# Gate and branch projections of a gated mixer, turned: tokens on the output partitions, 512 weight columns streaming, and the mixture transposed for the output projection

## The chip, the cores and the metric

The kernel runs on one core of one Trainium2 chip. The metric is the device time of one execution in microseconds (us), the median of three runs. Of the core's engines, TensorE (PE) multiplies and transposes, VectorE (DVE) and ScalarE (ACT) do the elementwise work, and SyncE (SP) issues the transfers of the weights. PSUM, into which TensorE writes, has eight banks of 128 partitions x 512 four-byte numbers.

## The reference

A trunk of two layers on 256 tokens of width 1024. Each layer has four residual steps, each behind a layer norm: a feed-forward half step, three gated mixers side by side, a cross attention to a memory, and a second feed-forward half step. The change is in the mixers:

```python
y_a = nsa_mixer(...)      # native sparse attention, 8 heads, width 512
y_b = hgrn2_mixer(...)    # gated linear recurrence, 4 heads, width 512
y_c = mla_mixer(...)      # latent attention, 8 heads, width 512
gates = sigmoid(merge.reshape(B, S, 3, D_MODEL))      # merge = x @ w_in's last 3072 columns
mixed = (gates[:, :, 0] * (y_a @ w_branch[l, 0]) + gates[:, :, 1] * (y_b @ w_branch[l, 1])
         + gates[:, :, 2] * (y_c @ w_branch[l, 2]))   # 256 x 1024
x = layer_norm(alpha * x + mixed @ w_out[l], ln_g[l, 1], ln_b[l, 1])
```

So each layer has three gate projections (256 x 1024 by 1024 x 1024), three branch projections (256 x 512 by 512 x 1024) and one output projection (256 x 1024 by 1024 x 1024) of the mixture.

## The kernel before

**Products.** Every factor is held as two fp32r tiles, a high part and the rest (names ending in h and l), and each product is three matmuls into the same PSUM region: high by high, high by low, low by high. They are issued by `mm3`, lines 127, 128 and 129, so each of these lines does a third of almost every product. Weights come in blocks of 128 x 1024 (512 KB): SP loads `raw` (5 buffers), ScalarE rounds it to `wh` (line 77) and VectorE makes the rest, `wl` (line 78), with 4 buffers each. VectorE so has one 128x1024 instruction for every block that TensorE works through.

**Gates and branches.** `merge(i, fc)` computes 128 of the 1024 gate columns of mixer i (0 is a, 1 is b, 2 is c): eight steps over k, the weight tile of 128 x 128 stationary and the 256 tokens of `xT` moving, so that the result `mg` has gate columns on the partitions and tokens along the row. ScalarE turns it to tanh in `th` (line 508). `branch(i, fp)` does the same for 256 of the 1024 columns of a branch projection (`br`, four steps over k), and VectorE forms (th + 1) * br; mixer b, the first, writes `mixed` (line 520), a and c go through `th` and are added (lines 523 and 524). With the last one, c, each 128 columns of `mixed` are at once halved and split into `mh` and `ml` (lines 528 and 529). In this layout `mixed` is already what the output projection needs as its stationary side. PSUM comes from two pools of four banks, `pacc` (mg, br of a and b, the output `y`) and `ppw` (scores, transposes, br of c).

**What stands around them.** Gates and branches are also the work that fills TensorE while the attention units wait for their softmax. They stand in the list `fillers`, and `fill(n)` takes the next n. Attention runs in 12 units (0 to 7 are heads of mixer a, 8 to 11 pairs of heads of c). The scores of a unit (`s`, lines 827 and 829) are issued two units ahead by `soft`, which also issues its softmax: VectorE masks and takes the maximum (line 427), ScalarE exponentiates (line 431), VectorE takes the reciprocal, applies the gate and scales `p` (lines 433, 435, 438). `unit(u, n)` then is:

```python
fill(n)                        # n = FILLS[u]
pT = flip(ahead.pop(0))        # six transposes of p (line 446), copies of them
if u == 0: ...                 # two transposes of scm (line 950), copied to pc
ahead.append(soften_a(u + 2))  # the scores of the unit after next
values_a(u, pT)                # oa <- pc, vc (line 841) and pT, vs (line 456)
```

`scm` is the softmax over compressed keys, for all heads at once, from `psc` (line 927), through VectorE's lines 929 to 940. The order of the text isn't the order on the engines: a scheduler lays each engine's instructions out ahead of the run, by times that it estimates.

**The tail of the mixers.** After unit 11 and the remaining fillers come `branch(2, fp)` for fp 0 to 3, two gates of c between them, and `nat_out`, the output projection: `y` in four banks, `mh` stationary and 512 columns of `w_out` moving, eight steps over k. `load_mem` loads the next step's memory beside it, with VectorE's `memT` (line 78, 128x512).

Of the kernel before, what the change touches and what calls it, by code (L numbers as in the profile page):

```python
# [30 lines left out]
ROPE_THETA = 500000.0  # L31
NEG = -1e30
TRAIL = 3
FILLS = (7, 0, 0, 0, 1, 2, 2, 2, 4, 4, 4, 0)
LEVELS = (4, 8, 16, 32, 64)
C_ID, C_CAUS, C_BASE, C_HM, C_CM, C_CM1, C_INV, C_END = 0, 128, 384, 448, 456, 488, 520, 536

# [2 lines left out]
def trunk(ctx, tc, a, out):  # L40
# [90 lines left out]
    def cut(hl, *idx):  # L131
        return tuple(t[idx] for t in hl)
# [331 lines left out]
    def mixer(l, xT, first, pre):  # L464
# [27 lines left out]
            return yh[name]  # L492


        order = "bac"
        mixed = []
        th = {}

        def merge(i, fc):
            ps = pacc([P, S], "mg")  # L500
            mode_b(ps, wblock(a["winb"][l, 8 + i * 8 + fc]), xT)
            if order[-1] == "abc"[i]:
                if fc % 4 == 0:
                    th[i] = big([P, 4, S], name="th")
                th[i, fc] = th[i][:, fc % 4, :]
            else:
                th[i, fc] = wk.tile([P, S], F32, tag="s", name="th", bufs=3)
            A.activation(th[i, fc], ps, AF.Tanh, scale=0.5)

        def branch(i, fp):  # L510
            w = wblock(a["wbr"][l, i, fp])
            res = []
            for u in range(2):
                fc = fp * 2 + u
                ps = (ppw if order[-1] == "abc"[i] else pacc)([P, S], "br")
                mode_b(ps, cut(w, slice(None), slice(u * 512, (u + 1) * 512)), yh["abc"[i]], 4)
                if order[0] == "abc"[i]:
                    if fc % 4 == 0:
                        mixed.append(big([P, 4, S], name="mixed"))
                    V.scalar_tensor_tensor(mixed[fc // 4][:, fc % 4, :], th[i, fc], 1.0, ps, op0=ALU.add, op1=ALU.mult)  # L520
                    continue
                m = mixed[fc // 4][:, fc % 4, :]
                V.scalar_tensor_tensor(th[i, fc], th[i, fc], 1.0, ps, op0=ALU.add, op1=ALU.mult)
                V.tensor_tensor(m, m, th[i, fc], op=ALU.add)
                if order[-1] == "abc"[i]:
                    mh = wk.tile([P, S], F32R, tag="gh", name="mh", bufs=4)
                    ml = wk.tile([P, S], F32R, tag="gl", name="ml", bufs=4)
                    A.activation(mh, m, AF.Copy, scale=0.5)
                    V.scalar_tensor_tensor(ml, m, 0.5, f(mh), op0=ALU.mult, op1=ALU.subtract)
                    res.append((mh, ml))  # L530
            return res

        def gated(i):
            u = []
            for fp in range(4):
                u += [lambda fp=fp: merge(i, fp * 2), lambda fp=fp: merge(i, fp * 2 + 1), lambda fp=fp: branch(i, fp)]
            return u

        fillers = []
# [222 lines left out]
            V.scalar_tensor_tensor(hx, u, 1.0, hx, op0=ALU.add, op1=ALU.mult)  # L762
            gel.append(hx)

        fillers += [lambda fc=fc: merge(2, fc) for fc in range(6)]
        compress(0)
        hgrn_out(0)
        blocks(1)
# [204 lines left out]
        memT = [load_mem(0)]  # L973

        ys = [[pacc([P, 512], "y") for _ in range(2)] for _ in range(NT)]
        mx = []
        for fp in range(4):
            mx += branch(2, fp)
            if fp == 0:
                merge(2, 6)  # L980
                merge(2, 7)
            if fp == 2:
                nat_out(ys, [(wblock(a["wo_mix"][l, k]), mx[k], k) for k in range(2)], KD)
        w = [wblock(a["wo_mix"][l, k]) for k in range(2, 8)]
        with tc.issue_after(latest[0].ins):
            nat_out(ys, [(w[k - 2], mx[k], k) for k in range(2, 4)], KD)
        memT.append(load_mem(1))
        nat_out(ys, [(w[k - 2], mx[k], k) for k in range(4, 8)], KD, True)
        return ys, nxt, memT


# [161 lines left out]
def _layout(d):  # L1153
    sizes = [512] + [128] * 6 + [24] + [512] * 4 + [384, 256, 32, 3072]
    at = np.concatenate([[0], np.cumsum(sizes)])
    (q, kc, vc, ks, vs, kw, vw, gate, bq, bf, bi, bg, cq, ckv, kr, mg) = [
        slice(int(at[n]), int(at[n + 1])) for n in range(16)]
    L = DEPTH
    w_in = d["w_in"]

    def cols(*s):
        return np.concatenate([w_in[:, :, x] for x in s], -1)

    def stationary(w, kchunks):
# [12 lines left out]
    o["x"] = x2  # L1177
    o["xT"] = x2.reshape(S, KD, P).transpose(2, 1, 0)
    o["memT"] = d["mem"].reshape(S, KD, P).transpose(2, 1, 0)
    o["pos"] = d["positions"].reshape(NT, P).T  # L1180
    o["ln_g"], o["ln_b"] = d["ln_g"], d["ln_b"]
    o["w13"] = np.stack([stationary(d["ffn_w1"], KD), stationary(d["ffn_w3"], KD)], 3)
    o["w2"] = d["ffn_w2"].reshape(L, 2, NF, P, D)
    o["winb"] = stationary(cols(bf, bq, mg), KD)
    o["wina"] = pairs(cols(bi, bg, q, kc, vc, ks, vs, kw, vw, ckv), 512)
    o["winc"] = pairs(cols(cq, gate, kr), 440)[:, 0]
    o["cw1"] = d["nsa_cmp_w1"].reshape(L, 2, 4, 4, P, 256).transpose(0, 1, 2, 4, 3, 5).reshape(L, 2, 4, P, 1024)
    w2 = d["nsa_cmp_w2"].reshape(L, 2, 2, P, 64).transpose(3, 0, 1, 2, 4)
    o["w2k"] = np.concatenate([w2[:, :, 0], w2[:, :, 0]], -1)
    o["w2v"] = w2[:, :, 1]  # L1190
    vec = np.zeros((P, L, 38), np.float32)
    vec[:, :, 0] = d["hgrn_norm_g"].T
    vec[:, :, 1:4] = d["mla_q_norm_g"].reshape(L, 3, P).transpose(2, 0, 1)
    vec[:, :, 4:6] = d["mla_kv_norm_g"].reshape(L, 2, P).transpose(2, 0, 1)
    pe = d["nsa_cmp_pos"].reshape(L, 2, 16, P).transpose(3, 0, 1, 2)
    vec[:, :, 6:38] = pe.reshape(P, L, 32)
    o["vec"] = vec
    o["lbl"] = d["hgrn_lb_logits"].reshape(L, 4, P).transpose(2, 0, 1)
    o["uq"] = d["mla_w_uq"].reshape(L, 3, P, 768)
    o["ukv"] = d["mla_w_ukv"].reshape(L, 2, P, 1024)  # L1200
    o["wbr"] = stationary(d["w_branch"], 4).reshape(L, 3, 4, 2, P, 512).transpose(0, 1, 2, 4, 3, 5).reshape(
        L, 3, 4, P, 1024)
    o["wo_mix"] = d["w_out"].reshape(L, KD, P, D)
    o["wq"] = stationary(d["xa_wq"], KD)
    o["wk"] = stationary(d["xa_wk"], KD)
    o["wv"] = pairs(d["xa_wv"], 512)
    o["wo"] = d["xa_wo"].reshape(L, KD, P, D)
    o["cst"], o["msk"] = _constants()
    return {k: np.ascontiguousarray(v) for k, v in o.items()}
# [20 lines left out]
```

## Time and profile before

| | |
|---|---|
| runs (us) | 1584.76, 1585.52, 1585.53; median 1585.52 |
| the profiled execution's own time (us) | 1585.19 |
| its span in the profile (us) | 1583.4 |
| TensorE busy in the span | 1565.3 us, 99% |
| VectorE, ScalarE | 66%, 52% |
| mean granted TensorE clock | 0.998 of full speed |

The span runs from the first to the last instruction that the profiler recorded; the execution's own time lies 1.8 us above it. Matmuls are pipelined: the time given for one is from its start to its end, and the next starts before that end, so that what one costs is the distance of two starts. Busy time is the union of such spans.

### The profile page before, as it was taken

The numbers are of one execution on the slowest core, as the hardware profiler recorded it, in microseconds if no ns is written. First come the engines' busy times: TensorE is split into PE (matmuls) and PEld (weight loads), VectorE is DVE, ScalarE is ACT, GpSimd is POOL, SyncE is SP. The second block draws the span as 40 slices with busy tenths as digits, with TensorE's granted clock in tenths as the row PEclk, the third lists the DMA queues.
The fourth block names the chain that finished last, engine by engine and source line by source line (L and its number), as shares of the span: only waits on it lengthen the run. The fifth ranks groups of instructions, "written<-read, shape, count | busy, mean of one in ns | idle before, by whom it ended". The sixth has DMA issues, their size and how long they took to land.

```text
span 1583.4 us, 27651 instructions
## 1 busy us (share of the span) xinstructions
PE 1565.3 (99%) x11056; PEld 1445.4 (91%) x11056; DVE 1038.0 (66%) x1821; ACT 828.2 (52%) x1398; POOL 34.4 (2%) x32
## 2 busy tenths in 40 slices
PE   9999999999999999999999999999999999999997
PEld 8999998898998989999999999988989989899996
DVE  5586568778776775555565555787786776655555
ACT  5455365566664555444444454656575545454443
POOL 0000000000000000000000000000000000000000
PEclk9999999999999999999999999999999999999999
DMA  8668455562555464666636676356524545455662
GB/s 287 213 205 274 147 160 166 173 221 77 173 176 171 147 229 132 188 199 224 212 122 187 199 223 214 120 167 192 191 86 164 170 148 198 162 179 186 186 185 76
DMA packets 81200, 282.27 MB, mean 178 GB/s; under 512 B 9392, under 2 KB 10672, under 8 KB 81072
## 3 DMA queue, kind: packets, MB, share of 16 engines
q1 hardware_dynamic: 81072, 280.52, 55.3%
q8 instruction: 86, 1.41, 0.4%
q14 instruction: 42, 0.34, 0.1%
HBM read 279.44 MB, written 1.05 MB: 177 GB/s over the span
## 4 chain that ended last, share of the span: by engine, by line
PE 97%; DVE 1%; ACT 1%; issue 0%; DMA 0%; POOLq 0%; POOL 0%; DVEq 0%; SPq 0%; ACTq 0%
PE up L127 10%; PE up L128 10%; PE up L129 10%; PE y L127 7%; PE y L128 7%; PE y L129 7%; PE mg L127 3%; PE mg L128 3%; PE mg L129 3%; PE pn L127 3%; PE pn L128 3%; PE pn L129 3%; PE br L127 2%; PE br L129 1%; PE br L128 1%; PE up L138 1%
## 5 line engine op out<-in xcount | busy, mean ns | idle before, releaser
L78 DVE TENSOR_TENSOR wl<-raw,wh 128x1024 fp32r<-128x1024 f32 (+3 forms) x490 | 584.7, 1200 | 368.2 <-ACT wh L77 366.5
L77 ACT ACTIVATE wh<-raw 128x1024 fp32r<-128x1024 f32 (+3 forms) x490 | 504.8, 1039 | 512.3 <-issue 234.5
L128 PE MATMUL up<-xTl,wh 128*128 128x256 f32 x1360 | 385.7, 284 | 0.0
L127 PE MATMUL up<-xTh,wh 128*128 128x256 f32 x1360 | 384.9, 284 | 0.4 <-ACT xTh L77 0.4
L129 PE MATMUL up<-xTh,wl 128*128 128x256 f32 x1360 | 384.9, 283 | 0.0
L127 PEld LDWEIGHTS up<-xTh,wh 128*128 128x128 f32 x1360 | 261.4, 192 | 3.9 <-ACT xTh L77 1.1
L128 PEld LDWEIGHTS up<-xTl,wh 128*128 128x128 f32 x1360 | 261.7, 192 | 3.0
L129 PEld LDWEIGHTS up<-xTh,wl 128*128 128x128 f32 x1360 | 261.3, 192 | 0.0
L128 PE MATMUL y<-wl,gh 128*128 128x512 f32 x352 | 137.2, 392 | 0.0
L127 PE MATMUL y<-wh,gh 128*128 128x512 f32 x352 | 136.8, 392 | 0.0
L129 PE MATMUL y<-wh,gl 128*128 128x512 f32 x352 | 135.6, 389 | 0.0
L127 PE MATMUL mg<-xTh,wh 128*128 128x256 f32 x384 | 110.0, 286 | 0.0
L128 PE MATMUL mg<-xTl,wh 128*128 128x256 f32 x384 | 109.2, 284 | 0.0
L129 PE MATMUL mg<-xTh,wl 128*128 128x256 f32 x384 | 108.9, 284 | 0.0
L129 PEld LDWEIGHTS y<-wh,gl 128*128 128x128 f32 x352 | 66.1, 188 | 14.3
L127 PEld LDWEIGHTS y<-wh,gh 128*128 128x128 f32 x352 | 66.3, 189 | 11.7
L128 PEld LDWEIGHTS y<-wl,gh 128*128 128x128 f32 x352 | 66.4, 189 | 11.0
L127 PEld LDWEIGHTS mg<-xTh,wh 128*128 128x128 f32 x384 | 73.5, 191 | 1.9 <-issue 1.1
L127 PE MATMUL pn<-wh,xTh 128*128 128x512 f32 (+1 forms) x192 | 74.6, 388 | 0.0
L128 PE MATMUL pn<-wl,xTh 128*128 128x512 f32 (+1 forms) x192 | 74.3, 387 | 0.0
L129 PE MATMUL pn<-wh,xTl 128*128 128x512 f32 (+1 forms) x192 | 74.1, 386 | 0.0
L128 PEld LDWEIGHTS mg<-xTl,wh 128*128 128x128 f32 x384 | 73.5, 191 | 0.4 <-issue 0.3
(411 smaller groups left out, 2839.9 us busy)
## 6 DMA issues: line engine op xcount, KB each, us to landing
raw<-in_w_dram SPq DMA_DIRECT2D x260, 512.0 KB, 3.9
raw<-in_winb_dram SPq DMA_DIRECT2D x64, 512.0 KB, 4.1
raw<-in_wina_dram SPq DMA_DIRECT2D x40, 512.0 KB, 3.7
raw<-in_wbr_dram SPq DMA_DIRECT2D x24, 512.0 KB, 4.1
raw<-in_wk_dram SPq DMA_DIRECT2D x16, 512.0 KB, 3.3
raw<-in_cw_dram SPq DMA_DIRECT2D x16, 512.0 KB, 3.6
raw<-in_wv_dram SPq DMA_DIRECT2D x16, 512.0 KB, 3.4
raw<-in_wq_dram SPq DMA_DIRECT2D x16, 512.0 KB, 4.3
```

The source lines that it names most:

```text
L77: i = A.activation(h, src, AF.Copy)
L78: j = V.tensor_tensor(l, src, f(h), op=ALU.subtract)
L127: T.matmul(o, lhs[0], rhs[0], start=start, stop=False)
L128: T.matmul(o, lhs[0], rhs[1], start=False, stop=False)
L129: latest[0] = T.matmul(o, lhs[1], rhs[0], start=False, stop=stop)
L138: T.matmul(o, w[i][:, k * P:(k + 1) * P], rhs[j][:, k], start=n + k == 0, stop=(n, k) == (2, nk - 1))
```

## The change

Gates and branches change sides. The stationary side of each matmul is now 128 tokens of `xT` (or of `yh`) and the moving side 512 columns of the weights, so that `mg` and `br` have tokens on the partitions and 512 columns along the row, a whole bank. A gate projection goes in two halves g of 512 columns, with four units q of two steps over k each; its two banks (one for each 128 tokens) are held through the four units. A branch projection has two units for each g. `th` and `mixed` become 128x512 pieces; `th` of a and b comes from the pool `half` instead of a ring of its own. The mixture, now with tokens on the partitions, is turned by `turned(g)`: eight 128x128 transposes, and the split into `mh` and `ml` from their result. The weights of gates and branches are laid out anew in DRAM, in blocks of the same size and number. The table `FILLS` counts in the new units, all eight gate units of c are taken ahead of the attention units, and the tail is written in a new order.

```diff
-FILLS = (7, 0, 0, 0, 1, 2, 2, 2, 4, 4, 4, 0)
+FILLS = (6, 0, 0, 0, 0, 2, 2, 2, 4, 4, 4, 0)
...
-        def merge(i, fc):
-            ps = pacc([P, S], "mg")
-            mode_b(ps, wblock(a["winb"][l, 8 + i * 8 + fc]), xT)
...
+        def product(o, lhs, k, w, kk, first, last_k):
+            for t in range(NT):
+                mm3(o[t], cut(lhs, slice(None), k, slice(t * P, (t + 1) * P)),
+                    cut(w, slice(None), slice(kk * 512, (kk + 1) * 512)), first, last_k)
+
+        def merge(i, g, q):
+            if q == 0:
+                pg[i, g] = [pacc([P, 512], "mg") for _ in range(NT)]
+            w = wblock(a["wing"][l, i * 2 + g, q])
+            for kk in range(2):
+                k = q * 2 + kk
+                product(pg[i, g], xT, k, w, kk, k == 0, k == KD - 1)
+            if q == 3:
...
+                for t in range(NT):
+                    A.activation(th[i, g][t], pg[i, g][t], AF.Tanh, scale=0.5)
+
+        def branch(i, g, q):
+            if q == 0:
+                pg[i, g] = [(ppw if order[-1] == "abc"[i] else pacc)([P, 512], "br") for _ in range(NT)]
+            w = wblock(a["wbr"][l, i, g, q])
+            for kk in range(2):
+                k = q * 2 + kk
+                product(pg[i, g], yh["abc"[i]], k, w, kk, k == 0, k == 3)
+            if q == 0:
+                return
...
+            for t in range(NT):
+                m, u = mixed[g][:, t, :], th[i, g][t]
                 if order[0] == "abc"[i]:
...
+                    V.scalar_tensor_tensor(m, u, 1.0, pg[i, g][t], op0=ALU.add, op1=ALU.mult)
                     continue
...
+                V.scalar_tensor_tensor(u, u, 1.0, pg[i, g][t], op0=ALU.add, op1=ALU.mult)
+                V.tensor_tensor(m, m, u, op=ALU.add)
+
+        def turned(g):
+            hl = big([P, 4, S], F32R, name="mh"), big([P, 4, S], F32R, name="ml")
+            for t in range(NT):
+                pt = ppw([P, 4, P], "pt")
+                for c in range(4):
+                    T.transpose(pt[:, c, :], mixed[g][:, t, c * P:(c + 1) * P], ident)
+                evac_hl(*[x[:, :, t * P:(t + 1) * P] for x in hl], pt, 0.5)
+            return [cut(hl, slice(None), c) for c in range(4)]
...
-        fillers += [lambda fc=fc: merge(2, fc) for fc in range(6)]
+        fillers += [lambda g=g, q=q: merge(2, g, q) for g in range(2) for q in range(4)]
...
+        branch(2, 0, 0)
+        branch(2, 0, 1)
+        branch(2, 1, 0)
+        mx = turned(0)
+        branch(2, 1, 1)
+        w = [wblock(a["wo_mix"][l, k]) for k in range(4)]
+        nat_out(ys, [(w[k], mx[k], k) for k in range(2)], KD)
+        mx += turned(1)
+        nat_out(ys, [(w[k], mx[k], k) for k in range(2, 4)], KD)
         memT.append(load_mem(1))
-        nat_out(ys, [(w[k - 2], mx[k], k) for k in range(4, 8)], KD, True)
+        w += [wblock(a["wo_mix"][l, k]) for k in range(4, 8)]
+        nat_out(ys, [(w[k], mx[k], k) for k in range(4, 8)], KD, True)
```

What the scheduler makes of it stands at two places otherwise than before, which are called the head and the tail here.

**The head**, where layer 0's unit 0 begins. First TensorE before, at the scores of unit 1 (s_3987 and s_3988; pieces of br between):

```order
L827 MATMUL s_3987<-kh,qs 128x512
L827 MATMUL s_3987<-kl,qs 128x512
L127 MATMUL br<-yh,wh 128x256
L128 MATMUL br<-yl,wh 128x256
L129 MATMUL br<-yh,wl 128x256
L127 MATMUL br<-yh,wh 128x256
L128 MATMUL br<-yl,wh 128x256
L129 MATMUL br<-yh,wl 128x256
L829 MATMUL s_3988<-kh,qs 128x256
L829 MATMUL s_3988<-kl,qs 128x256
```

Behind these rows stand 15 more of br and 24 of mg, which are the last ahead of unit 0's flip; the rows that follow are (scores s_4260 and s_4261 belong to unit 2):

```order
L127 MATMUL mg<-xTh,wh 128x256
L128 MATMUL mg<-xTl,wh 128x256
L129 MATMUL mg<-xTh,wl 128x256
L446 MATMUL pt<-cst,p 128x128 x6
L950 MATMUL pt<-cst,scm 128x128 x2
L827 MATMUL s_4260<-kh,qs 128x512
L827 MATMUL s_4260<-kl,qs 128x512
```

TensorE after, at the same place (s_3924 and s_3925 are the scores of unit 0, s_3947 and s_3948 of unit 1, s_4105 of unit 2; psc are the scores of the compressed keys):

```order
L830 MATMUL pt<-cst,kd 128x128 x4
L944 MATMUL psc<-kc_blk,qtu 128x32 x8
L844 MATMUL s_3924<-kh,qs 128x512
L846 MATMUL s_3925<-kh,qs 128x256
L846 MATMUL s_3925<-kl,qs 128x256
L844 MATMUL s_3924<-kl,qs 128x512
L844 MATMUL s_3947<-kh,qs 128x512
L844 MATMUL s_3947<-kl,qs 128x512
L846 MATMUL s_3948<-kh,qs 128x256
L846 MATMUL s_3948<-kl,qs 128x256
L446 MATMUL pt<-cst,p 128x128 x6
L967 MATMUL pt<-cst,scm 128x128 x2
```

The pieces of br and mg between the scores and the flip are gone from here: 24 matmuls of br stand directly ahead of these rows, and the four transposes of kd and all of psc come behind them.

VectorE after, at the same place; it works through these rows before it comes to unit 0's reductions (L427, named ISA in this listing), between which those of unit 1 stand too:

```order
L536 SCALAR_TENSOR_TENSOR mixed<-th,br 128x512 x2
L78 TENSOR_TENSOR wl<-raw,wh 128x1024
L946 TENSOR_TENSOR scm<-psc,cst 128x128
L78 TENSOR_TENSOR kl<-pt,kh 128x4x128
L946 TENSOR_TENSOR scm<-psc,cst 128x128
L427 ISA p,nm<-s_3925,cst 128x128
```

Two half-size rows of `mixed` stood here before; now two of 128x512 from the br matmuls just named stand ahead of the low part kl of the last keys and of both rows of scm.

**The tail**, where the output projection of layer 0's mixers begins. TensorE before:

```order
L127 MATMUL br<-yh,wh 128x256
L128 MATMUL br<-yl,wh 128x256
L129 MATMUL br<-yh,wl 128x256
L127 MATMUL y<-wh,mh 128x512
L128 MATMUL y<-wl,mh 128x512
L129 MATMUL y<-wh,ml 128x512
```

TensorE after, from the last four matmuls of the branches, one for each of their banks:

```order
L129 MATMUL br_5134<-wh_5155,yl_4450 128x512
L129 MATMUL br_5135<-wh_5155,yl_4450 128x512
L129 MATMUL br_5176<-wh_5213,yl_4450 128x512
L129 MATMUL br_5177<-wh_5213,yl_4450 128x512
L546 MATMUL pt_5198<-cst_82,mixed_4087 128x128 x4
L546 MATMUL pt_5205<-cst_82,mixed_4087 128x128 x4
L127 MATMUL y_5130<-wh_5235,mh_5196 128x512
L128 MATMUL y_5130<-wl_5236,mh_5196 128x512
L127 MATMUL y_5131<-wh_5235,mh_5196 128x512
L128 MATMUL y_5131<-wl_5236,mh_5196 128x512
L546 MATMUL pt_5284<-cst_82,mixed_4672 128x128 x4
```

The transposes of the mixture, mixed_4087 for the first 512 columns and mixed_4672 for the others, follow the last matmul of the branches with nothing between.

VectorE after, between those last matmuls of br and the split of the first transposes:

```order
L538 SCALAR_TENSOR_TENSOR th_3683<-th_3683,br_5134 128x512
L538 SCALAR_TENSOR_TENSOR th_3683<-th_3683,br_5135 128x512
L538 SCALAR_TENSOR_TENSOR th_3897<-th_3897,br_5176 128x512
L538 SCALAR_TENSOR_TENSOR th_3897<-th_3897,br_5177 128x512
L78 TENSOR_TENSOR memT_5323<-ld_5324,memT_5322 128x512
L539 TENSOR_TENSOR mixed_4087<-mixed_4087,th_3683 128x512
L78 TENSOR_TENSOR memT_5323<-ld_5328,memT_5322 128x512
L539 TENSOR_TENSOR mixed_4087<-mixed_4087,th_3683 128x512
L78 TENSOR_TENSOR wl_5248<-raw_5246,wh_5247 128x1024
L539 TENSOR_TENSOR mixed_4672<-mixed_4672,th_3897 128x512 x2
L78 TENSOR_TENSOR wl_5254<-raw_5252,wh_5253 128x1024
L97 SCALAR_TENSOR_TENSOR ml_5197<-pt_5198,mh_5196 128x4x128
```

Before, VectorE's rows between br and y took 128x256 pieces one at a time, as each 128 columns of the branches ended; now four of 128x512, two pieces of `memT` and a weight block stand among the additions.

## Rows read from the trace of the kernel before

**Rows 1.** Page: busy time, share and instructions; chain that ended last, by engine.
```profile
PE 1565.3 (99%) x11056; PEld 1445.4 (91%) x11056; DVE 1038.0 (66%) x1821; ACT 828.2 (52%) x1398; POOL 34.4 (2%) x32
...
PE 97%; DVE 1%; ACT 1%; issue 0%; DMA 0%; POOLq 0%; POOL 0%; DVEq 0%; SPq 0%; ACTq 0%
```

**Rows 2.** Groups of instructions on PE: count, busy us, mean ns, idle before.
```profile
L127 PE MATMUL mg<-xTh,wh 128*128 128x256 f32 x384 | 110.0, 286 | 0.0
...
L127 PE MATMUL br<-yh,wh 128*128 128x256 f32 x192 | 54.1, 287 | 0.0
```

**Rows 3.** PE in order of time (start us, duration us), one stretch of gates.
```profile
342.72 0.28 PE L128 MATMUL mg<-xTl,wh 128*128 128x256 f32 x1
...
344.40 0.28 PE L127 MATMUL mg<-xTh,wh 128*128 128x256 f32 x1
```

**Rows 4.** The same view, one stretch of a projection with tokens on the partitions.
```profile
275.75 0.39 PE L127 MATMUL pn<-wh,xTh 128*128 128x512 f32 x1
...
278.49 0.39 PE L127 MATMUL pn<-wh,xTh 128*128 128x512 f32 x1
```

**Rows 5.** The same view: a gate's matmul behind an attention score's, and the next.
```profile
365.10 0.36 PE L128 MATMUL mg<-xTl,wh 128*128 128x256 f32 x1
365.30 0.28 PE L129 MATMUL mg<-xTh,wl 128*128 128x256 f32 x1
```

**Rows 6.** The same view: eight transposes, and the matmul behind them.
```profile
518.35 1.03 PE L318 MATMUL pst<-cst,xn 128*128 128x128 f32 x8
519.14 0.48 PE L128 MATMUL mv<-al,memT 128*128 128x512 f32 x1
```

**Rows 7.** PE's waits over the execution: us in total, times, longest.
```profile
PE oa L841 <- DVE pc L951: 1.9, 2, 1.0
...
PE pt L446 <- DVE p L438: 0.6, 2, 0.3
```

**Rows 8.** PE in order of time at layer 0's head; idle before it in brackets.
```profile
367.06 0.28 PE L829 MATMUL s<-kl,qs 128*128 128x256 f32 x1
...
373.72 0.85 PE L446 MATMUL pt<-cst,p 128*128 128x128 f32 x6 [0.29 <-DVE p L438]
```

**Rows 9.** DVE in order of time at layer 0's head: reductions, then scaling.
```profile
367.15 0.42 DVE L427 CUSTOM_DVE_ANT_0 p<-s,cst 128x256 f32<-128x256 f32 x1 [0.64 <-PE s L827]
...
367.50 0.42 DVE L427 CUSTOM_DVE_ANT_0 p<-s,cst 128x256 f32<-128x256 f32 x1
...
367.84 0.29 DVE L427 CUSTOM_DVE_ANT_0 p<-s,cst 128x128 f32<-128x128 f32 x1
...
368.05 0.29 DVE L427 CUSTOM_DVE_ANT_0 p<-s,cst 128x128 f32<-128x128 f32 x1
...
372.43 0.61 DVE L438 TENSOR_SCALAR p<-p,w 128x256 f32<-128x256 f32 x2
372.95 0.42 DVE L938 TENSOR_TENSOR scm<-scm,cm 128x256 f32<-128x256 f32 x1
373.29 0.48 DVE L438 TENSOR_SCALAR p<-p,w 128x128 f32<-128x128 f32 x2
```

**Rows 10.** Groups of instructions on DVE, by shape.
```profile
L78 DVE TENSOR_TENSOR wl<-raw,wh 128x1024 fp32r<-128x1024 f32 x464 | 564.6, 1223 | 358.1 <-ACT wh L77 356.7
...
L787 DVE SCALAR_TENSOR_TENSOR vc<-pv,cst 128x512 f32<-128x512 f32 x2 | 1.4, 692 | 1.6 <-PE pv L785 1.6
```

**Rows 11.** Last matmuls at layer 0's tail, in order of time.
```profile
497.57 0.28 PE L129 MATMUL br<-yh,wl 128*128 128x256 f32 x1
497.69 0.40 PE L127 MATMUL y<-wh,mh 128*128 128x512 f32 x1
```

**Rows 12.** The execution's last matmul; then windows behind it (busy us, PEclk, DMA).
```profile
1573.04 0.39 PE L129 MATMUL y<-wh,gl 128*128 128x512 f32 x1
...
1576.00:1577.00 1.00, 0.00 (x0) 0.00 (x0) 0.02 (x1) 0.94 (x2) 0.00 (x0) 0.80 1.01 387
1577.00:1578.00 1.00, 0.00 (x0) 0.00 (x0) 1.00 (x2) 0.00 (x0) 0.72 (x1) 0.50 0.07 27
```

More of the change, by code (lines that the diff above doesn't have):

```diff
@@ L497, in mixer @@
         th = {}
-        def merge(i, fc):
-            ps = pacc([P, S], "mg")
-            mode_b(ps, wblock(a["winb"][l, 8 + i * 8 + fc]), xT)
[L502 to L516, printed above, removed]
+        pg = {}
@@ new lines, in product @@
+        def product(o, lhs, k, w, kk, first, last_k):
[10 more added lines that the diff above has]
+            if q == 3:
+                if order[-1] == "abc"[i]:
+                    t2 = big([P, NT, 512], name="th")
+                    th[i, g] = [t2[:, t, :] for t in range(NT)]
+                else:
+                    th[i, g] = [half([P, 512], name="th") for t in range(NT)]
+                for t in range(NT):
+                    A.activation(th[i, g][t], pg[i, g][t], AF.Tanh, scale=0.5)
@@ new lines, in branch @@
+        def branch(i, g, q):
[7 more added lines that the diff above has]
+                return
+            if order[0] == "abc"[i]:
+                mixed.append(big([P, NT, 512], name="mixed"))
+            for t in range(NT):
+                m, u = mixed[g][:, t, :], th[i, g][t]
@@ L517, in branch @@
                 if order[0] == "abc"[i]:
-                    if fc % 4 == 0:
-                        mixed.append(big([P, 4, S], name="mixed"))
-                    V.scalar_tensor_tensor(mixed[fc // 4][:, fc % 4, :], th[i, fc], 1.0, ps, op0=ALU.add, op1=ALU.mult)
+                    V.scalar_tensor_tensor(m, u, 1.0, pg[i, g][t], op0=ALU.add, op1=ALU.mult)
                     continue
-                m = mixed[fc // 4][:, fc % 4, :]
-                V.scalar_tensor_tensor(th[i, fc], th[i, fc], 1.0, ps, op0=ALU.add, op1=ALU.mult)
@@ L524, in branch @@
[L524 to L531, printed above, removed]
+                V.scalar_tensor_tensor(u, u, 1.0, pg[i, g][t], op0=ALU.add, op1=ALU.mult)
@@ L533, in gated @@
         def gated(i):
             u = []
-            for fp in range(4):
-                u += [lambda fp=fp: merge(i, fp * 2), lambda fp=fp: merge(i, fp * 2 + 1), lambda fp=fp: branch(i, fp)]
+            for g in range(2):
+                u += [lambda g=g, q=q: merge(i, g, q) for q in range(4)] + [lambda g=g, q=q: branch(i, g, q) for q in range(2)]
             return u
@@ L975, in mixer @@
         ys = [[pacc([P, 512], "y") for _ in range(2)] for _ in range(NT)]
[L976 to L986, printed above, removed]
+        branch(2, 0, 0)
[7 more added lines that the diff above has]
+        nat_out(ys, [(w[k], mx[k], k) for k in range(2, 4)], KD)
         memT.append(load_mem(1))
-        nat_out(ys, [(w[k - 2], mx[k], k) for k in range(4, 8)], KD, True)
+        w += [wblock(a["wo_mix"][l, k]) for k in range(4, 8)]
+        nat_out(ys, [(w[k], mx[k], k) for k in range(4, 8)], KD, True)
         return ys, nxt, memT
@@ L1183, in _layout @@
     o["w2"] = d["ffn_w2"].reshape(L, 2, NF, P, D)
-    o["winb"] = stationary(cols(bf, bq, mg), KD)
+    o["winb"] = stationary(cols(bf, bq), KD)
+    o["wing"] = pairs(cols(mg), 512)
     o["wina"] = pairs(cols(bi, bg, q, kc, vc, ks, vs, kw, vw, ckv), 512)
@@ L1200, in _layout @@
     o["ukv"] = d["mla_w_ukv"].reshape(L, 2, P, 1024)
-    o["wbr"] = stationary(d["w_branch"], 4).reshape(L, 3, 4, 2, P, 512).transpose(0, 1, 2, 4, 3, 5).reshape(
-        L, 3, 4, P, 1024)
+    o["wbr"] = d["w_branch"].reshape(L, 3, 2, 2, P, 2, 512).transpose(0, 1, 5, 2, 4, 3, 6).reshape(L, 3, 2, 2, P, 1024)
     o["wo_mix"] = d["w_out"].reshape(L, KD, P, D)
```

## The prediction

> **What bounds the kernel now.** I read the page first, for who works: TensorE is busy for 99% of the span, and 97% of the chain that ended last is TensorE's own instructions [rows 1]. The groups come next: 3 x 384 matmuls of mg and 3 x 192 of br, none with an idle time before it [rows 2]. Their durations overlap, so I read prices as distances of starts. Fourteen steps of mg take 344.40 - 342.72 = 1.68 us, 0.120 each [rows 3]; twelve of a projection that already has the new form (128x512) take 278.49 - 275.75 = 2.74, 0.228 each [rows 4]. Last come TensorE's waits: unit 0's flip waits 0.3 us in each layer, and oa a little under 1 us for pc [rows 7], 1.26 together. The output projection waits for nothing: y starts 0.12 us behind the last br, the normal distance [rows 11]. So the time is the sum of TensorE's distances plus a few waits, and the change is worth what it does to these two.
>
> **What the change removes.** 1728 matmuls at 0.120 are 207.4 us; 864 at 0.228 are 197.0. That is 10.4 us less. Where a piece of mg stands behind an attention score, its first distance is 0.20 instead of 0.12 [rows 5], and the listings of TensorE's order have 108 unbroken pieces of mg and br before and 54 after: 54 x 0.08 = 4.3 at most. I take 3.1, since some pieces began beside a neighbour of their own kind. Together -13.5 (bounds -10.4 and -14.7). The weight blocks stay the same in number and size, so ScalarE and VectorE prepare as much as before.
>
> **What it adds on TensorE.** Sixteen transposes a layer. Eight took 519.14 - 518.35 = 0.79 us, with a 1.03 duration for the group [rows 6]; 0.107 each by these two is what I take between 0.10 and 0.13: 32 x 0.107 = +3.4.
>
> If nothing else changed, this would be 10 us faster. But gates and branches are also the cover under which the softmax runs, and the listings show that cover gone at two places.
>
> **The head.** Before, 6.4 us lie between the last score of unit 0 (ends 367.34) and its flip (373.72), filled with mg, br and unit 1's scores, and only 0.3 of them are idle [rows 8]. After, only unit 1's four scores stand there. The chain, from H, the end of the last br ahead of it: four transposes (0.43) and eight psc matmuls (an estimate of 0.12 each, that of a 256-wide one) take TensorE to H + 1.4. VectorE meanwhile has its list. A 128x256 instruction takes 0.42 but the next starts 0.35 behind it (367.15 to 367.50), a 128x128 one 0.21 behind (367.84 to 368.05) [rows 9], so I subtract 0.07 from each duration: 128x512, as in L787, is 0.62 and a weight block 1.15 [rows 10]. Two mixed (to H + 1.45, the first can begin 0.2 early), a weight block (2.6), scm (2.8), kl (3.5), scm (3.7). The scores need kh and kl of the last keys and a bank that scm frees, so these (4 x 0.228 + 4 x 0.12 = 1.4 us) wait some 1.65 us on the way and end at H + 4.5. VectorE is free for unit 0's reductions at H + 3.7. There now stand the eight reductions of both units, 4 x 0.35 + 4 x 0.21 = 2.24 [rows 9], three passes of scm (1.0, at the 0.34 between 372.95 and 373.29), two small rows (0.15, an estimate) and the scaling of p, 0.52 + 0.40 [rows 9]: 4.3 in sum, so p is ready at H + 8.0. ScalarE's exponentials run beside it. The flip waits 8.0 - 4.5 = **3.5**. It takes 0.7, and the scm transposes then need four small rows, two passes of scm and the scaling of unit 1's p, which stands ahead: 2.0 and a little for the hand-over, to H + 10.2, a wait of 1.5. In sum 1.65 + 3.5 + 1.5 = 6.65 us against 1.26 before: +5.4 a layer. Unit 1's flip and values follow with no fillers either; I add 1.0 (between 0 and 2). Two layers: **+13**. Bounds: if VectorE has its list done earlier (mixed at once, the weight block later), the scores don't wait and the reductions start 1.3 earlier: 3.7 in all, +2.4 a layer; with ScalarE's exponentials in series and the full wait of unit 1, +8.5. I take nearer the middle, since the listing fixes the order and every row in it hangs on H.
>
> **The tail.** T is when TensorE is through with the last br. All four br banks get their last matmul within the last four, because these need the low part yl of the last heads. VectorE then has, in order, rows of 128x512 at 0.62 [rows 10]: four products of th and br, the first from T - 0.45, to T + 2.0; memT, 2.65; the first addition, T + 3.3. There the first four transposes may start: **wait 3.3**. memT again and the second addition, 4.55: wait 0.85 after the 0.43 of the first four. Then a weight block and two additions, for the transposes of the other half (wait 0.45, since four matmuls of y stand between), another block and the split, for the first low-part matmul (0.6). Sum 5.2 a layer; before 0 [rows 11]. Two layers: **+10.4**. Bounds: with the memory pieces and the blocks out of the way early, two products, an addition and the split remain exposed, 1.5; with every wait in full and ScalarE's split behind its own blocks, 6.5.
>
> **Sum.** The profiled execution took 1585.2, 0.3 below the median of the runs. 1585.2 - 13.5 + 3.4 + 13 + 10.4 = 1598.5; I say 1599. With one place at its middle and the other at a bound the case spans 1592 to 1608.
>
> **Rivals.**
>
> *The clock falls in the new waits.* At the end of the execution the last matmul ends at 1573.43, TensorE is idle from there on, and the granted clock is 0.80 in the window 1576 to 1577 and 0.50 in the next [rows 12]: it went from 2.4 to 1.2 GHz in that idle time. The waits at the flip and at the first transposes, 3.5 and 3.3 by my sums, are idle times of nearly that length. If the clock falls in one, the matmuls behind it have double distances until it comes back. No row of this trace shows how long that lasts in mid-kernel; its cost lies between nothing, if the fall comes after the wait is over, and as much again as the wait itself, 2 to 4 us. I take 2.5, near the lower of these, for four falls: 1598.5 + 10 = 1608, at most 1598.5 + 16 = 1614. Against it: the waits may be shorter, and TensorE may come to them later. Chance 0.2.
>
> The Trainium skill has this rule (TensorE: Matmul & The Clock Gate, HAM oscillation — how this bites in real kernels): where the idle times between bursts of matmuls are long enough, the engine is set back to half clock in each of them, and pays for it every time. The trace agrees at its one long idle time [rows 12]; by that rule the sum would be this rival's, by the mean clock of 0.998 over the whole execution mine.
>
> *Short chains.* VectorE runs ahead at both places: +2.4 and +1.5 a layer: 1585.2 - 10.1 + 7.8 = 1582.9, up to 1586 with a little of each wait left. Within 0.2% of before, which is 3.2 us, about what a measurement of this kernel can tell from no change. Chance 0.12.
>
> *Faster.* VectorE's rows at both places run under matmuls that stand ahead of them, so that the waits are hidden: 1585.2 - 13.5 + 3.4 = 1575, or 1577 with 1 us a layer. The point that decides: faster by over 0.2% needs all new waits together under (10.1 - 3.2) / 2 = 3.4 us a layer. For it speaks that VectorE was busy for only 66% of the span [rows 1]; against it, that the rows in question depend on the last br itself at the tail, so that at least a product, an addition and a split lie behind T. Chance 0.1.
>
> **How the numbers follow.** My forecast has 0.58, the clock 0.2, short chains 0.12, faster 0.1. The first two are slower than 1588.7: 0.78. The range reaches from 1582, just under the short chains' figure, to 1611, inside the clock's; beyond lie the faster case and some 0.07 of the clock's. The likeliest case's own range is 1592 to 1608.
>
> **What would show it.** In the trace after: distances of 0.228 for mg and br of 128x512, so some 197 us for both; a wait of TensorE at L446 for L438 of 3 us or more in each layer with one of 1 to 2 us at L967 behind it, and one at L546 for L539 of about 3.3 with shorter ones after it. TensorE's idle time would be some 22 us larger than before. Granted clock under 1.00 in the windows behind these waits would show the rival with the clock. I am wrong if these waits come out under 3.4 us a layer together, which would mean that VectorE's rows were done earlier than I place them, or if the distances of 0.228 don't hold where the weights are the moving side and come from freshly written tiles.

## The result, and the profile after

The changed kernel takes 1611.32 us (median of four runs, 1609.63 to 1613.65) against 1585.18 before: a ratio of 1.0166, with a 95% interval of 1.0148 to 1.0184. It is slower, as forecast, but by 26 us instead of 14, and the time lies 0.3 us above the range. The profiled execution took 1609.82 us, 24.6 more than the profiled one of before.

The page after, its busy line and its chain; they answer to [rows 1]:

```profile
PE 1573.2 (98%) x10224; PEld 1410.0 (88%) x10224; DVE 1035.5 (64%) x1773; ACT 827.9 (51%) x1366; POOL 36.2 (2%) x32
...
PE 94%; DVE 4%; ACT 1%; issue 1%; DMA 0%; POOLq 0%; POOL 0%; DVEq 0%; SPq 0%; ACTq 0%
```

TensorE issues 832 matmuls fewer and is yet busy for 8 us longer, and 4% of the chain are now VectorE's. So there are waits, and beside them TensorE's own work became slower somewhere. The mean granted clock says where: 0.989, against 0.998.

The groups of gates, branches and new transposes, which answer to [rows 2] (count, busy us, mean ns, idle before):

```profile
L127 PE MATMUL mg<-wh,xTh 128*128 128x512 f32 x192 | 75.4, 401 | 4.1 <-DVE vm L908 4.1
...
L127 PE MATMUL br<-wh,yh 128*128 128x512 f32 x96 | 39.1, 411 | 0.0
...
L546 PE MATMUL pt<-cst,mixed 128*128 128x128 f32 x32 | 7.0, 358 | 6.8 <-DVE mixed L539 6.7
```

The counts are halved, as planned, and the new transposes wait. So do gates, which no step of the prediction had. TensorE's waits, which answer to [rows 7] (us in total, times, longest):

```profile
PE pt L546 <- DVE mixed L539: 6.7, 3, 3.1
PE pt L446 <- DVE p L438: 6.4, 3, 3.3
PE mg L127 <- DVE vm L908: 4.1, 2, 2.0
...
PE pt L967 <- DVE scm L957: 0.8, 1, 0.8
...
PE s L846 <- DVE scm L946: 0.6, 2, 0.3
```

Layer 0's head on TensorE, which answers to [rows 8], from the last score of unit 1 to the scm transposes:

```profile
375.56 0.41 PE L846 MATMUL s<-kl,qs 128*128 128x256 f32 x1
378.60 1.51 PE L446 MATMUL pt<-cst,p 128*128 128x128 f32 x6 [2.62 <-DVE p L438]
380.89 0.66 PE L967 MATMUL pt<-cst,scm 128*128 128x128 f32 x2 [0.77 <-DVE scm L957]
```

The flip at layer 1's head:

```profile
1174.82 1.52 PE L446 MATMUL pt<-cst,p 128*128 128x128 f32 x6 [3.29 <-DVE p L438]
```

And VectorE at the same place (compare [rows 9]):

```profile
370.69 1.28 DVE L536 SCALAR_TENSOR_TENSOR mixed<-th,br 128x512 f32<-128x512 f32 x2
371.89 1.22 DVE L78 TENSOR_TENSOR wl<-raw,wh 128x1024 fp32r<-128x1024 f32 x1
...
373.83 0.28 DVE L946 TENSOR_TENSOR scm<-psc,cst 128x128 f32<-128x128 f32 x1
374.02 0.28 DVE L427 CUSTOM_DVE_ANT_0 p<-s,cst 128x128 f32<-128x128 f32 x1
...
377.66 0.99 DVE L438 TENSOR_SCALAR p<-p,w 128x256 f32<-128x256 f32 x4
```

VectorE has no gap of 0.1 us from the first row to the last. The matmuls behind the last br start at 370.44, which is H: the weight block starts at H + 1.45, the reductions at H + 3.6, and p is scaled at H + 8.1. So it is the length of VectorE's list that sets when the flip may start.

The tail of layer 0, the last four of br and the transposes behind them, against the unbroken 0.12 us of [rows 11]; then VectorE between them:

```profile
496.93 1.07 PE L129 MATMUL br<-wh,yl 128*128 128x512 f32 x4
501.09 2.32 PE L546 MATMUL pt<-cst,mixed 128*128 128x128 f32 x8 [3.10 <-DVE mixed L539]
```

```profile
497.35 2.48 DVE L538 SCALAR_TENSOR_TENSOR th<-th,br 128x512 f32<-128x512 f32 x4 [1.33 <-PE br L129]
499.75 0.69 DVE L78 TENSOR_TENSOR memT<-ld,memT 128x512 fp32r<-128x512 f32 x1
500.35 0.69 DVE L539 TENSOR_TENSOR mixed<-mixed,th 128x512 f32<-128x512 f32 x1
```

Eight transposes took 2.32 us here where eight took 1.03 before [rows 6]. They ran at half clock. Windows of 2 us (busy us of each engine, then PEclk, DMA share and GB/s), which answer to [rows 12]:

```profile
374.00:376.00 2.00, 1.98 (x5) 1.39 (x5) 1.95 (x13) 1.65 (x7) 0.00 (x0) 0.52 0.78 240
...
412.00:414.00 2.00, 2.00 (x6) 1.52 (x6) 2.00 (x9) 0.88 (x4) 0.00 (x0) 0.50 0.77 227
...
502.00:504.00 2.00, 1.91 (x7) 1.57 (x7) 2.00 (x4) 1.15 (x2) 0.00 (x0) 0.50 0.03 8
...
1174.00:1176.00 2.00, 1.18 (x6) 1.16 (x7) 2.00 (x11) 1.02 (x5) 0.00 (x0) 0.50 0.00 0
...
1206.00:1208.00 2.00, 0.96 (x4) 0.83 (x5) 2.00 (x8) 1.59 (x7) 0.00 (x0) 1.00 0.86 272
```

Read in half-microsecond windows, the clock is at 1.2 instead of 2.4 GHz in five stretches: from 374.1 to 384.3 (layer 0's head), 411.6 to 415.0 (a gate behind the wait for vm), 500.4 to 507.2 (layer 0's tail), 1172.8 to 1179.6 (layer 1's head) and 1295.7 to 1299.1 (layer 1's tail).

**An account of the difference**, from the first matmul of the mixers (zf) to the first of the cross attention's query (qx), both layers added (a matmul costs the distance to the next start less the idle time; the half-clock excess is that distance less the mean one of the same tile and shape at full clock in the same trace):

| both layers, us | before | after | difference | predicted |
|---|---|---|---|---|
| TensorE's work at full clock | 617.6 | 614.6 | -3.1 | -10.1 |
| idle | 3.4 | 19.6 | +16.2 | +23.4 |
| excess at half clock | 0 | 11.2 | +11.2 | 0 (rival: +10) |
| sum | 621.0 | 645.3 | +24.3 | +13.3 |

### The profile page after: what moved, and what is told of

It reads as the page before. It is cut to its first block, busy times and chain, and to the rows that moved or that the text cites. A ratio compares the mean times of both kernels' runs of the same rounds, so it can differ in the third digit from the quotient of the medians.

```text
span 1608.0 us, 25891 instructions
## 1 busy us (share of the span) xinstructions
PE 1573.2 (98%) x10224; PEld 1410.0 (88%) x10224; DVE 1035.5 (64%) x1773; ACT 827.9 (51%) x1366; POOL 36.2 (2%) x32
## 4 chain that ended last, share of the span: by engine, by line
PE 94%; DVE 4%; ACT 1%; issue 1%; DMA 0%; POOLq 0%; POOL 0%; DVEq 0%; SPq 0%; ACTq 0%
PE up L127 10%; PE up L128 10%; PE up L129 10%; PE y L127 7%; PE y L128 7%; PE y L129 7%; PE mg L127 3%; PE mg L128 3%; PE mg L129 3%; PE pn L127 3%; PE pn L129 3%; PE pn L128 3%; PE br L127 1%; PE br L128 1%; PE br L129 1%; PE up L138 1%
## 5 line engine op out<-in xcount | busy, mean ns | idle before, releaser
L127 PE MATMUL mg<-wh,xTh 128*128 128x512 f32 x192 | 75.4, 401 | 4.1 <-DVE vm L908 4.1
L128 PE MATMUL mg<-wl,xTh 128*128 128x512 f32 x192 | 76.2, 397 | 0.0
L129 PE MATMUL mg<-wh,xTl 128*128 128x512 f32 x192 | 75.6, 394 | 0.0
L431 ACT ACTIVATE p<-p,nm 128x128 f32<-128x128 f32 (+1 forms) x96 | 42.5, 445 | 26.8 <-DVE nm L427 26.8
L279 POOL TENSOR_TENSOR rs<-rs,mhalf 128x1 f32<-128x1 f32 x16 | 23.7, 1482 | 1317.8 <-DVE rs L278 1317.8
```

Of the source, the lines that this page charges most:

```text
L127: T.matmul(o, lhs[0], rhs[0], start=start, stop=False)
L128: T.matmul(o, lhs[0], rhs[1], start=False, stop=False)
L129: latest[0] = T.matmul(o, lhs[1], rhs[0], start=False, stop=stop)
L279: G.tensor_tensor(dst, dst, mhalf[:, 0:dst.shape[1]], op=ALU.pow)
L431: A.activation(p[:, i, c], p[:, i, c], AF.Exp, scale=-1.0, bias=nm[:, t, i:i + 1], accum_out=w[:, t, i:i + 1])
```

## The experiments

Two theories stood against each other. **Cover**: the change takes away the matmuls under which VectorE's chains ran, TensorE waits for these chains, and the clock falls in or near the waits. **Form**: the wide pieces themselves cost more, wherever they stand. All versions below are of the changed kernel, but for one; the kernel before ran on the same chip each time, at 1584.8 to 1585.1 us.

**1. Cover for the head.** `latest[0]` is the last score of unit 1 here.

```diff
         def unit(u, n):
-            fill(n)
+            with tc.issue_after(latest[0].ins) if u == 0 else nullcontext():
+                fill(n)
```

> Edit: the changed kernel, with the six filler units of unit 0 queued on TensorE behind the scores of units 0 and 1, so that 72 matmuls of mg and br stand between these scores and the flip. Cover theory: the waits at the head (2.6 and 0.8 us in layer 0, 3.3 and 0.5 in layer 1, 0.4 at the scores of each) and the half clock there (3.1 and 2.3 us of excess) come from the missing cover; they go, and the kernel is 10 to 13 us faster than the changed one, near 1599 us. Rival, form theory: the loss lies in the wider pieces themselves; the waits move to the place ahead of the scores, from which the units were taken, and the time stays within 3 us of 1610.

1608.35 us (1607.18 to 1610.23), ratio 1.0149 [1.0135, 1.0163]: 3 us less than the changed kernel, and the two intervals overlap. The 10 to 13 us of the cover theory did not come. The head did what the cover theory says, with 0.6 us a layer left at the flip and no half clock there. But a new wait stood where the units were taken from, and the time stayed within 3 us of 1610, both as the rival expected (TensorE's waits of this version):

```profile
PE pv L802 <- DVE gd L798: 5.7, 2, 2.9
...
PE pt L446 <- DVE p L438: 1.2, 2, 0.6
```

The wait moved with the order of the same pieces, so cover is a stock: what is moved to one place is missing at another.

**2. Cover for the tail.**

```diff
         branch(2, 0, 0)
         branch(2, 0, 1)
-        branch(2, 1, 0)
+        with tc.issue_after(latest[0].ins):
+            branch(2, 1, 0)
+            branch(2, 1, 1)
         mx = turned(0)
-        branch(2, 1, 1)
...
-        mx += turned(1)
+        with tc.issue_after(latest[0].ins):
+            mx += turned(1)
```

> Edit: the changed kernel, with the last two units of c's branch (24 matmuls) queued behind the last matmul of the first two, and the transposes of the second half of the mixture queued behind the output projection's first steps. Cover theory: 5.5 us of br cover VectorE's products and additions for the first half; the waits at the transposes (3.1 us in layer 0, 3.1 and 0.6 in layer 1) and the half clock there (2.8 and 1.3 us of excess) go, and the kernel is 9 to 11 us faster than the changed one, near 1600 us. Rival: TensorE now waits before, for the low part yl of the last heads, by 1 to 3 us a layer, since the br that filled that time stand behind it; then 3 to 5 us faster at most.

1606.13 us (1605.54 to 1606.85), ratio 1.0134 [1.0120, 1.0148]: 5.2 us faster, half of the expected. The transposes no longer wait and the clock doesn't fall there, but the next step of the chain now shows, ScalarE's split of the transposed mixture:

```profile
PE y L127 <- ACT mh L96: 3.1, 2, 1.6
...
PE y L129 <- DVE ml L97: 0.9, 2, 0.5
```

The rival's wait for yl did not come.

**3. No gate behind pq.**

```diff
-FILLS = (6, 0, 0, 0, 0, 2, 2, 2, 4, 4, 4, 0)
+FILLS = (6, 0, 0, 0, 0, 0, 3, 3, 4, 4, 4, 0)
```

> Edit: the changed kernel with FILLS (6, 0, 0, 0, 0, 0, 3, 3, 4, 4, 4, 0), so that no gate unit stands at unit 5, where the four banks of pq hold the whole pool. Cover theory: the two waits of mg for VectorE's vm (2.0 us each) come from the banks and go, with the half clock behind the one in layer 0 (1.6 us): 4 to 6 us faster than the changed kernel, near 1605 us. Rival: unit 5 needs that cover and waits as long at its flip, time unchanged.

1608.69 us (1608.21 to 1612.37), ratio 1.0154 [1.0141, 1.0168], not told apart from the changed kernel: the expected 4 to 6 us did not come. The wait kept its length and went to the next that asks for a bank of that pool:

```profile
PE oa L858 <- DVE vm L908: 4.1, 2, 2.0
```

So the wait is for the banks that pq holds until VectorE has taken vm out of them, not for anything in the gates.

**4. Waits kept busy.** Twelve matmuls of 128x512, which nothing reads, in the waits of head and tail; the lines below are the tail's, with `branch(2, 1, 1)` set ahead of them, where the scheduler had put it already.

```diff
+        branch(2, 1, 1)
+        with tc.issue_after(latest[0].ins):
+            for _ in range(12):
+                T.matmul(ys[0][0], xT[0][:, 0, 0:P], xT[0][:, 0:2, :], start=True, stop=True)
         mx = turned(0)
-        branch(2, 1, 1)
```

> Edit: the changed kernel with 12 matmuls of 128x512, whose result nothing reads, behind the scores of unit 1 and 12 behind the last br, 2.7 us each, inside the waits that are there anyway. If the clock falls because TensorE idles there, the half clock at the tails (2.8 and 1.3 us of excess) and behind the flips (3.1 and 2.3) goes and the waits stay as long in sum with the spare work: 6 to 9 us faster than the changed kernel, near 1603 us. If it falls because of the narrow matmuls and transposes ahead of the scores, or at random, the falls stay and the time is unchanged or a little longer.

1606.77 us (1605.04 to 1608.36), ratio 1.0137 [1.0124, 1.0151]: 4.5 us faster with 48 more matmuls. Four spare pieces of 2.75 us took 7.5 us out of the idle time, so that idle time and spare work together grew by 3.5; the excess at half clock fell from 11.2 to 2.6. The mean granted clock was 0.996 to 0.998 in all four runs, against 0.986 to 0.989 in the four of the changed kernel. Layer 1's head, its spare piece (the last 11 of its 12 matmuls), the flip and the window:

```profile
1169.72 2.65 PE L968 MATMUL spare<-xTh 128*128 128x512 f32 x11
1172.94 0.85 PE L446 MATMUL pt<-cst,p 128*128 128x128 f32 x6 [0.56 <-DVE p L438]
```

```profile
1172.00:1174.00 2.00, 1.23 (x8) 0.64 (x6) 2.00 (x11) 1.37 (x7) 0.00 (x0) 1.00 0.00 0
```

Six transposes take 0.85 us there, instead of 1.52 at the same flip of the changed kernel. So at both tails and at layer 1's head the clock did not fall once the idle time was filled. The fall at layer 0's head (374.1) was there before the spare piece began, and stayed, as did the one behind the wait for vm in layer 0.

**5. The head's cover split**: of the six units only the two branch units behind the scores, the four gate units ahead of them (`scored` is the last score of unit 1).

```diff
         def unit(u, n):
-            fill(n)
+            if u == 0:
+                fill(4)
+                n -= 4
+            with tc.issue_after(scored.ins) if u == 0 else nullcontext():
+                fill(n)
```

> Edit: the changed kernel, with only the two branch units of unit 0's six filler units queued behind the scores of units 0 and 1 (24 matmuls, 5.5 us), and the four gate units left ahead. Cover theory: 5.5 us cover the flip's 2.6 and 3.3 us and the scm transposes, and the gates still cover pv, which waited 2.9 us a layer with all six moved: 10 to 12 us faster than the changed kernel, near 1600 us. Rival, the cover is used up: a wait of 2 to 3 us a layer opens at pv or at the scores again, near 1607 us.

1606.65 us (1603.63 to 1607.78), ratio 1.0133 [1.0119, 1.0147]: 4.7 us faster, the rival's figure. pv waits no more, unit 0's flip 0.3 us, later flips 0.8 us at most, but a third place opens, the transposes of the last keys, from where the br were taken:

```profile
PE pt L830 <- DVE qs L827: 2.8, 2, 1.4
```

**6. One gate half early**, between the two groups of pq.

```diff
-FILLS = (6, 0, 0, 0, 0, 2, 2, 2, 4, 4, 4, 0)
+FILLS = (6, 0, 0, 0, 4, 0, 0, 2, 4, 4, 4, 0)
```

> Edit: the changed kernel with FILLS (6, 0, 0, 0, 4, 0, 0, 2, 4, 4, 4, 0), so that the four units of one gate half run between the two groups of pq, as one gate unit did in the kernel before, instead of behind the second. Cover theory: the wait of 2.0 us a layer for the banks of pq goes, since what comes next on TensorE are scores and transposes in the other pool: 4 to 6 us faster than the changed kernel, near 1606 us. Rival: whatever asks first for a bank of that pool waits as long, time unchanged.

1603.73 us (1603.08 to 1605.81), ratio 1.0122 [1.0107, 1.0138]: 7.6 us faster, more than the 4 to 6 expected. No wait for vm is left in its trace, 4.1 us; with it the half clock behind that wait went (8.4 us of excess in all instead of 11.2).

**7. All of it**: edits 5 and 6, and a tail in which the first transposes stand between the last two branch units (`turn[0]` is the last of these transposes; the second half's are queued as in 2).

```diff
         branch(2, 0, 0)
         branch(2, 0, 1)
-        branch(2, 1, 0)
-        mx = turned(0)
-        branch(2, 1, 1)
+        with tc.issue_after(latest[0].ins):
+            branch(2, 1, 0)
+        with tc.issue_after(latest[0].ins):
+            mx = turned(0)
+        with tc.issue_after(turn[0].ins):
+            branch(2, 1, 1)
```

> Edit: the changed kernel with both edits just named, and a tail in which 12 of the last matmuls of br stand ahead of the first transposes of the mixture and 12 behind them, and the transposes of the second half stand behind the first steps of the output projection. Cover theory: the waits at head, pq and tail go but for about 1 us a layer, and with them nearly all the half clock; left is TensorE's own work, 3.1 us less than before by the accounts of the two traces, and the waits of the kernel before, 1.3 us a layer, are gone too: 1580 to 1586 us. Rival, form theory: the wide pieces cost what they cost wherever they stand, 1595 us or more.

1587.35 us (1586.08 to 1591.56, eleven runs), ratio 1.0017 [1.0008, 1.0026]: 24 us faster than the changed kernel, with the same pieces, layout and count of matmuls. The form theory, 1595 or more, falls. The time lies 1.4 us above the range expected by the cover theory, because more waits are left than the 1 us a layer that it allowed: in its profile the mixers are idle for 7.7 us, instead of 19.6 in the changed kernel. No matmul of them runs at half clock there (mean clock 0.998). Its largest waits:

```profile
PE pt L832 <- DVE qs L829: 2.8, 2, 1.4
PE pt L446 <- DVE p L438: 1.4, 2, 0.8
PE s L848 <- DVE pT L450: 1.3, 1, 1.3
```

**8. The converse**: the kernel before, with unit 0's units all ahead of the scores.

```diff
-FILLS = (7, 0, 0, 0, 1, 2, 2, 2, 4, 4, 4, 0)
+FILLS = (0, 0, 0, 0, 1, 2, 2, 2, 4, 4, 4, 0)
...
-        ahead = [soften_a(0), soften_a(1)]
+        fill(7)
+        with tc.issue_after(latest[0].ins):
+            ahead = [soften_a(0), soften_a(1)]
```

> Edit: the kernel before, with all seven filler units of unit 0 queued ahead of the scores of units 0 and 1, so that nothing stands between these and the flip; pieces and layout stay those of before. Cover theory: the flip now waits 2 to 3.5 us in each layer instead of 0.3, and the clock falls in some of these waits: 4 to 10 us slower than before, 1589 to 1595 us. Form theory: no change, 1585 us.

1592.13 us (1591.26 to 1592.51), ratio 1.0043 [1.0031, 1.0056]: 7 us slower, with the old pieces. The flip waits 3.84 us in each layer, and the clock falls behind it:

```profile
373.00 0.28 PE L829 MATMUL s<-kl,qs 128*128 128x256 f32 x1
377.13 0.85 PE L446 MATMUL pt<-cst,p 128*128 128x128 f32 x6 [3.84 <-DVE p L438]
```

```profile
378.00:380.00 2.00, 2.00 (x10) 1.81 (x9) 2.00 (x10) 0.50 (x2) 0.00 (x0) 0.53 0.00 0
```

**9 and 10. More cover for the head.** As 7, with four gate units of mixer a taken from units 8 to 10 to the head, where two stand ahead of the scores and two behind.

```diff
-        fillers += gated(1)
+        ones = gated(1)
+        fillers += ones[:4] + [lambda q=q: merge(0, 0, q) for q in range(4)] + ones[4:]
...
-                fillers += gated(0)
+                fillers += gated(0)[4:]
...
-FILLS = (6, 0, 0, 0, 4, 0, 0, 2, 4, 4, 4, 0)
+FILLS = (10, 0, 0, 0, 4, 0, 0, 2, 3, 3, 2, 0)
```

> Edit: as the version with all three edits (1587.35 us), and in addition one gate half of mixer a (48 matmuls) is taken from the units 8 to 10 to the head, two of its units ahead of the last keys' transposes, where a wait of 1.4 us a layer stands, and two behind the scores. Cover theory: the waits at the head (1.4, 0.5 to 1.3 and 0.6 to 1.1 us a layer) go; units 8 to 10 had no wait and can spare it: 4 to 5 us faster, 1582 to 1584 us, so a little faster than the kernel before. Rival: cover is short everywhere, and 2 us a layer open in units 8 to 11: 1587 us again.

1584.13 us (1582.83 to 1585.07, eleven runs), ratio 0.9993 [0.9984, 1.0002], not told apart from the kernel before.

> Edit: the same with FILLS 2, 3, 3 instead of 3, 3, 2 in units 8 to 10. Cover theory: head as in the other, and the last units better covered; within 1 us of it, the better of the two under 1584 us. Rival: waits in unit 8 or 9 of 1 us a layer or more.

1581.16 us (1580.45 to 1583.57, eight runs), ratio 0.9978 [0.9968, 0.9988]: 4 us faster than the kernel before, and 30 faster than the changed one, and 3 us faster than the first of the two, where at most 1 was expected. In the first of the two an oc of unit 8 to 11 waits 0.6 us a layer; in the second the mixers are idle for 1.6 us a layer, 0.1 less than before, most of it in the waits below, and its clock is 0.998:

```profile
PE pt L446 <- DVE p L438: 1.2, 2, 0.6
...
PE pt L548 <- DVE mixed L539: 0.6, 2, 0.3
```

**11. The tail's chain on VectorE in another order.** `added` is VectorE's last addition.

```diff
-        memT = [load_mem(0)]
...
+        with tc.issue_after(added[0].ins):
+            memT = [load_mem(0)]
         w = [wblock(a["wo_mix"][l, k]) for k in range(4)]
```

> Edit: the changed kernel, with VectorE's two memT rows of the tail queued behind its last addition; VectorE's order then is three products, an addition, a product, a weight block, an addition. Reading of the tail as one chain on VectorE: the first transposes wait 2.0 us instead of 3.1 (one product and one memT fewer ahead), the second about 1.9 instead of 0.1 to 0.6 (a product and a block between); the sum changes by less than 1 us a layer, the time by less than 3 us. If instead TensorE waits for something else there, the first wait stays at 3.1.

1610.91 us (1609.93 to 1611.04), ratio 1.0162 [1.0148, 1.0176], no change. The waits at the transposes moved as VectorE's rows did:

```profile
499.38 0.66 PE L547 MATMUL pt<-cst,mixed 128*128 128x128 f32 x4 [1.22 <-DVE mixed L540]
501.71 1.12 PE L547 MATMUL pt<-cst,mixed 128*128 128x128 f32 x4 [1.68 <-DVE mixed L540]
```

The first is shorter than expected (2.0), because the branches' matmuls came in another order too; it is not 3.1, so it was VectorE's chain that TensorE waited for.

## Why the prediction was wrong

**What failed** is the choice between the forecast and its first rival. The prediction saw that the clock might fall in the new waits, gave it 0.2, and put it at nothing in the sum. It fell, and cost 11.2 us, near the rival's 10. Its two flips and two tails make up 9.5 of this, as the rival had it, though at layer 0's head the clock fell ahead of the wait; the fifth fall, behind the wait for vm, was not foreseen. The rows for the rival were there: [rows 12] show a fall in an idle time about as long as the waits that were forecast (the last matmul ends at 1573.43, and the window 1576 to 1577 has 0.80). The Trainium skill says that an idle time which is long enough sets the engine back to half clock each time (TensorE: Matmul & The Clock Gate, HAM oscillation — how this bites in real kernels). Experiment 8 agrees, where it fell behind a wait of 3.84 us in both layers; in the changed kernel it also fell at shorter ones, 3.1 us at both tails. With 1598.5 + 11.2 the sum would have been 1609.7. Four more terms were off, by +7.0 (work), -7.5 (head), -3.6 (tail) and +4.1 (a wait not foreseen), which happen to cancel:

- *Work of the pieces, -13.5 predicted.* The prices hold: 443.56 - 440.36 us for fourteen steps of mg below is 0.229 each, as in [rows 4]. But in the version of experiment 7, where the clock doesn't disturb the account, gates and branches cost 101.1 us a layer against 105.95: -9.7 for both. The halved number of pieces brought nothing, so the step that took it for a saving failed too. Of the 108 pieces before, 44 start behind the other of the two, mg behind br or br behind mg, at a mean 0.124 us, so almost free; only 64 start behind something else, and in the version of experiment 7 these are still 56. These cost on average 0.06 us more than the matmuls behind them there and 0.07 here (one of the new form: 440.05 to 440.36, 0.31 instead of 0.23), so that their sum is the same. And the scores, transposes and oc that now stand with other neighbours cost a net 1.3 us a layer more.

```profile
440.05 0.47 PE L127 MATMUL mg<-wh,xTh 128*128 128x512 f32 x1
440.36 0.39 PE L128 MATMUL mg<-wl,xTh 128*128 128x512 f32 x1
...
443.56 0.39 PE L127 MATMUL mg<-wh,xTh 128*128 128x512 f32 x1
```

- *Transposes, +3.4:* 1.72 a layer in experiment 7, so 3.4.
- *Head, +13:* the chain on VectorE was right to 0.1 us (p at H + 8.1, forecast 8.0). TensorE's side of it was not: the psc matmuls ran to H + 2.1 instead of 1.4, since there are 16 in the trace, so that the scores waited for 0.4 us and not 1.65; in layer 0 the scores also ended late, at half clock. So TensorE idled less: 3.8 and 4.2 us at the head, instead of 7.65 a layer (6.65, and 1.0 for what follows). Against 2.5 us for both layers before, this is +5.5.
- *Tail, +10.4:* the first wait is 3.1 instead of 3.3 in both layers; the shorter ones behind it, 1.9 in sum by the forecast, came to 0.1 and 0.55, for the most part since TensorE at half clock arrived later itself. +6.8.
- *A wait not foreseen, +4.1:* gates now take two banks for four units, where before one bank served one unit of 24 matmuls that fitted between the groups of pq. I had looked at the order, not at who holds the banks. Experiments 3 and 6 show it to be the banks.

**What held**: that the change loses by lost cover and not by its arithmetic. Experiments 7, 9 and 10 keep every piece of the new form and win the 24 to 30 us back by order alone; experiment 8 loses 7 us by order alone with the old form. The rivals of short chains and of a faster kernel fell: idle time grew by 8 us a layer, over the 3.4 that decided. That the whole loss hangs on the order, and not on the pieces, is shown, and the waits that open and close with it show that it is cover; how much of the clock's part comes at each place is not shown, since it varies (below).

## What to carry to other kernels

Where TensorE is busy all the time, independent matmuls are a stock of cover, and a change that makes them fewer, longer or hungrier for banks has to be judged by where the stock then stands: lay out the neighbour engine's chain from the last matmul it hangs on, in its queue order, and see what TensorE has meanwhile. An idle time of a few microseconds can cost more than itself, since the matmuls behind it may run at half clock for a while (here 19.6 us of idle time came with 11.2 of excess); put that into the sum, not only among the rivals. And a scheduler's order is no part of the form: the same pieces gave 1611 and 1581 us.

## What the runs showed of the hardware that was not expected

- The clock did not always need a long idle time. At layer 0's head it fell at 374.1, when TensorE had idled for 0.4 us in all since 370.4, and had done four transposes, 16 psc matmuls of 32 columns and three scores, and was at the fourth. With the same order of these matmuls it fell there too in the traces of experiments 2, 3, 4, 9 and 11, but not in 10, and in 6 only in the wait behind (377.2). The Trainium skill knows of a case like it (TensorE: Matmul & The Clock Gate, A second HAM failure mode: psum-queue depth-cycling), in which short idle times between groups of matmuls let the clock go up and down; whether here the narrow matmuls or the short waits do it, no run tells.
- The same wait of 2.03 us for vm, in the same order, had the clock fall behind it in layer 0 (window 412 to 414: 0.50) and not in layer 1 (1206 to 1208: 1.00). The number of falls so can differ between executions, and the time goes with the granted clock: the four runs of the changed kernel took 1609.6 and 1609.8 us at a mean clock of 0.989, and 1612.8 and 1613.7 at 0.986, and the fastest and slowest of experiment 7 took 1586.1 at 0.998 and 1591.6 at 0.994. A mean clock lower by 0.003 is some 10 us more of the execution at 1.2 GHz, and these cost 3.2 us, about a third; in the account above some 31 us at 1.2 GHz cost 11.2. So a difference of a few microseconds between two of these versions is partly one of falls.
- Once fallen, the clock stayed at half for 3.4 to 10.2 us in the changed kernel's trace, each time longer than TensorE's idle time ahead of the fall, while it was busy again for most of that time.
